# First two modulation vectors on TensorE in column tiles, and the order of work that follows from it

## The chip, the cores and the metric
The kernel runs on one core of a Trainium2 chip. The metric is the device time of one execution in microseconds (us). The engines are TensorE (PE for its matmuls, PEld for its weight loads), VectorE (DVE), ScalarE (ACT), GpSimd (POOL) and SyncE (SP), whose queue issues most transfers. Each engine works through its own instructions in order and waits on the others by semaphores.

## The reference, cut to what matters
One layer of a hybrid block over 1024 latent tokens and 256 context tokens, D = 1024, all in float32:

```
mods   = silu(c) @ ada_w + ada_b            # six vectors of 1024, for tokens; the same with c_ctx for the context
u      = rms_norm(x, ln1) * (1 + scale) + shift        # vectors 0 and 1; uc the same from ctx
z      = u @ w_in                            # S5, LRU, q, k, v, gates ... (5408 columns)
mixers : S5 scan, LRU (conv, two gated linear scans), GLA
out    : gated sum of branches @ w_out, residual, then norm, ConvFFN, residual, final norm
```

Vectors 0 and 1 are needed before the first projection can start, vectors 2 to 5 only after the mixers.

## The kernel before, in words
Everything is kept transposed: 128 channels on the partitions, tokens along the free axis, eight tiles k = 0 to 7 of 128 channels, and for the latent tokens two halves j of 512. Each float32 operand is split into a rounded part and a rest ("hi" and "lo", tiles `wh`/`wl` and `uh`/`ul`), and a product takes three matmuls: hi x hi, hi x lo, lo x hi.

**Start (lines 296 to 417, the table START on line 89).** The table is an order written out for all engines. Its steps: `x` loads half a tile of x (256 KB), `sq` squares it on ACT and adds it to a running sum, `rs` sums over channels on PE and takes the power -1/2, `rb` spreads the result over the partitions (line 272) and copies it to `rbc`. `a` loads 512 KB of `ada_w`; `ap` multiplies a block of 128 x 256 by one number of silu(c) and adds it up (L311, L313 on DVE, L307 and L309 on ACT and POOL); eight such products make the sums for the 128 channels of tile k, which `af` finishes on PE and DVE (L278, L318, L319). `xn` multiplies x by `rbc` (L381), `u` makes the hi part with scale and shift (L323) and writes the shifted x once more in full (L324), `ul` subtracts (L389). `g`/`gs` load and split the first weights. `m1`, `m2` and `mz` are the matmuls of three first blocks of 128 columns over all eight k and both halves (L395, L396, L402, and L283 to L285): 144 of 512 columns.

**Stream.** After that one generator, `proj_stream`, hands out all other projections. A `lat` block is 48 matmuls of 512 columns (L496 to L500), a `ctx` block 24 of 256. The call F(name) puts as many microseconds of the stream between two other pieces of PE's program as the table FILL says; `fill_until` runs it up to a marker. PE's order is that of the program; the other engines' order after the start is made by a scheduler from the dependencies.

**Context norm (lines 422 to 452).** The same norm for the context. The modulation of the context reads `ada_w` once more, and per k makes eight products on DVE, with 6 us of stream beside each k. Stream blocks handed out up to the marker "ctx": two gate blocks (lg), two q blocks, two g blocks.

**LRU (lines 899 to 964).** Two channel halves times two directions: six small matmuls each (L925), activations, scans, and per pass two rows of vectors 2 to 5: `ada_rows` (L474, 32 float32 matmuls of 32 x 128 in four column tiles), copied and turned into columns by `ada_cols` (L477, L483, L485). A row's weights are eight tiles of 256 KB, in one set of eight buffers. The stream gives k and v for the context and z; its marker "pc" ends the stage. Line 960 writes the LRU's result `yl`.

**S5 and on.** The S5 prologue on DVE, the decay logs of GLA, then S5, GLA, the merge, the FFN.

Of the kernel before, what the change touches and what calls it, by code (L numbers as in the profile page):

```python
# [20 lines left out]
KT = 8  # L21
# [17 lines left out]
def _parts(v, bits, n):  # L39
    out = []  # L40
    for _ in range(n):
# [21 lines left out]
FILL = {'ctx_a': [6.11],  # L63
        'ctx_b': [5.72],
        'ctx_k': [6.02, 6.02, 6.02, 6.02, 5.84, 6.02, 5.84, 6.02],
        'lru_a': [5.66],
        'lru_b': [1.42, 1.42, 1.34, 1.38, 1.04, 1.42, 1.48, 1.55, 1.42, 1.42, 1.38, 1.73, 1.42, 1.42, 1.42, 1.42, 1.78, 2.22, 1.42, 1.8, 1.42, 1.42, 1.92, 1.42],
# [19 lines left out]
ONPOOL = [('ap', 0, 3), ('ap', 0, 5), ('ap', 0, 6), ('ap', 1, 2), ('ap', 2, 7), ('ap', 3, 0), ('ap', 5, 3), ('ap', 7, 0), ('sq', 4, 0), ('sq', 5, 0), ('sq', 5, 1), ('sq', 6, 0), ('sq', 6, 1), ('xn', 0, 0), ('xn', 1, 0), ('xn', 2, 0), ('xn', 2, 1), ('xn', 5, 1), ('xn', 6, 0), ('xn', 7, 0), ('xn', 7, 1)]  # L87
ONDVE = [('ul', 6, 0), ('ul', 6, 1), ('ul', 7, 0), ('ul', 7, 1)]
START = [('x', 2, 1), ('x', 0, 0), ('sq', 0, 0), ('x', 5, 0), ('sq', 5, 0), ('x', 3, 0), ('sq', 3, 0), ('x', 4, 0), ('sq', 4, 0), ('x', 1, 0), ('sq', 1, 0), ('x', 7, 0), ('sq', 7, 0), ('x', 2, 0), ('sq', 2, 0), ('a', 0, 0), ('ap', 0, 0), ('ap', 0, 2), ('x', 6, 0), ('sq', 6, 0), ('ap', 0, 1), ('a', 0, 1), ('ap', 0, 4), ('a', 1, 0), ('ap', 0, 7), ('ap', 0, 6), ('ap', 0, 3), ('x', 1, 1), ('g', 0), ('x', 0, 1), ('x', 5, 1), ('ap', 0, 5), ('x', 3, 1), ('x', 4, 1), ('ap', 1, 0), ('ap', 1, 1), ('a', 1, 1), ('x', 6, 1), ('rs', 0), ('ap', 1, 2), ('g', 1), ('x', 7, 1), ('gs', 0, 0), ('gs', 0, 1), ('sq', 0, 1), ('sq', 1, 1), ('sq', 2, 1), ('sq', 4, 1), ('sq', 5, 1), ('ap', 1, 6), ('ap', 1, 4), ('af', 0), ('ap', 1, 3), ('sq', 6, 1), ('ap', 1, 7), ('rb', 0), ('xn', 0, 0), ('ap', 1, 5), ('sq', 3, 1), ('sq', 7, 1), ('a', 2, 0), ('a', 2, 1), ('ap', 2, 0), ('ap', 2, 2), ('ap', 2, 3), ('ap', 2, 1), ('ap', 2, 5), ('a', 3, 0), ('a', 3, 1), ('a', 4, 0), ('af', 1), ('ap', 2, 4), ('gs', 1, 0), ('gs', 0, 2), ('g', 2), ('gs', 1, 2), ('u', 0, 0), ('ul', 0, 0), ('a', 4, 1), ('rs', 1), ('ap', 2, 6), ('m1', 0, 0), ('a', 5, 0), ('xn', 1, 0), ('ap', 3, 0), ('ap', 3, 7), ('ap', 3, 5), ('ap', 3, 2), ('ap', 2, 7), ('a', 5, 1), ('gs', 1, 1), ('rb', 1), ('xn', 3, 0), ('m2', 0, 0), ('xn', 2, 0), ('af', 2), ('ap', 3, 4), ('xn', 2, 1), ('xn', 5, 0), ('ap', 3, 1), ('xn', 0, 1), ('u', 1, 0), ('m1', 1, 0), ('ul', 1, 0), ('u', 2, 0), ('ul', 2, 0), ('m1', 2, 0), ('ap', 3, 6), ('xn', 3, 1), ('u', 0, 1), ('m1', 0, 1), ('ul', 0, 1), ('m2', 2, 0), ('xn', 1, 1), ('u', 1, 1), ('ul', 1, 1), ('ap', 3, 3), ('a', 6, 0), ('a', 6, 1), ('ap', 4, 0), ('ap', 4, 5), ('ap', 4, 6), ('ap', 4, 7), ('ap', 4, 1), ('u', 2, 1), ('ul', 2, 1), ('af', 3), ('u', 3, 0), ('xn', 5, 1), ('ap', 4, 3), ('ap', 5, 0), ('ap', 5, 6), ('ap', 5, 1), ('ap', 5, 5), ('ap', 4, 4), ('ap', 5, 3), ('ul', 3, 0), ('xn', 4, 0), ('m2', 0, 1), ('gs', 2, 0), ('gs', 2, 2), ('u', 3, 1), ('ul', 3, 1), ('gs', 2, 1), ('m1', 1, 1), ('m1', 2, 1), ('m2', 2, 1), ('m2', 1, 1), ('ap', 4, 2), ('a', 7, 0), ('a', 7, 1), ('af', 4), ('u', 4, 0), ('xn', 4, 1), ('u', 4, 1), ('ap', 5, 7), ('m1', 3, 1), ('m1', 3, 0), ('m2', 3, 0), ('ap', 5, 4), ('ul', 4, 1), ('xn', 6, 1), ('ap', 5, 2), ('af', 5), ('u', 5, 0), ('m1', 4, 0), ('m2', 3, 1), ('ap', 6, 0), ('ap', 6, 4), ('ap', 6, 5), ('ap', 6, 2), ('m1', 5, 0), ('ap', 6, 7), ('m1', 4, 1), ('ap', 6, 6), ('ul', 4, 0), ('ap', 6, 3), ('ap', 6, 1), ('af', 6), ('ul', 5, 0), ('m2', 5, 0), ('m2', 1, 0), ('u', 5, 1), ('m1', 5, 1), ('ap', 7, 0), ('ap', 7, 7), ('ap', 7, 3), ('ap', 7, 1), ('ap', 7, 5), ('ap', 7, 6), ('xn', 6, 0), ('m2', 4, 0), ('ap', 7, 2), ('ul', 5, 1), ('g', 3), ('gs', 3, 0), ('gs', 3, 1), ('gs', 3, 2), ('u', 6, 0), ('m1', 6, 0), ('ap', 7, 4), ('af', 7), ('u', 6, 1), ('ul', 6, 1), ('m1', 6, 1), ('m2', 4, 1), ('m2', 6, 1), ('ul', 6, 0), ('m2', 6, 0), ('m2', 5, 1), ('xn', 7, 0), ('u', 7, 0), ('xn', 7, 1), ('u', 7, 1), ('ul', 7, 0), ('ul', 7, 1), ('mz',)]
# [22 lines left out]
def tile_kernel(tc, I, out, dbg=None):  # L112
# [140 lines left out]


# [39 lines left out]
    aws, raws, accs1, acs, dgs = {}, {}, {}, {}, {}  # L294

    def ada_load(k, i):

        aw = t0([128, 4, 256], "aw", 6)
        SY.dma_start(aw.rearrange("p k m -> p (k m)"), I["ada01"][k][:, i * 1024:(i + 1) * 1024])
        return aw  # L300

    def ada_prod(ac, kk, src, col, via):

        c = cs[:, kk, col:col + 1]
        if via:
            t = ac if kk == 0 else t0([128, 256], "at", 2)
            S.activation(t, src, AF.Copy, scale=c)  # L307
            if kk:
                G.tensor_tensor(ac, ac, t, OP.add)  # L309
        elif kk == 0:  # L310
            V.tensor_scalar(ac, src, c, None, OP.mult)  # L311
        else:
            V.scalar_tensor_tensor(ac, src, c, ac, OP.mult, OP.add)  # L313

    def ada_fin(k, ac, col, p):

        sums(p, ac, 2, 2 * k)
        V.scalar_tensor_tensor(mods[:, k, col, 0:1], p[:, 2 * k:2 * k + 1], ab1[:, k:k + 1], vc("ln1", k), OP.add, OP.mult)  # L318
        V.tensor_tensor(mods[:, k, col, 1:2], p[:, 2 * k + 1:2 * k + 2], vc("adab", k), OP.add)  # L319

    def u_hi(k, xk, col, oh):

        S.activation(oh, xk, AF.Identity, scale=mods[:, k, col, 0:1], bias=mods[:, k, col, 1:2])  # L323
        S.activation(xk, xk, AF.Identity, scale=mods[:, k, col, 0:1], bias=mods[:, k, col, 1:2])  # L324
# [4 lines left out]
    class Start:  # L329
# [4 lines left out]
        @staticmethod  # L334
        def a(k, i):
            aws[k, i] = ada_load(k, i)

        @staticmethod
        def g(kp):
            raws[kp] = wraw(I["g1"][kp])  # L340

        @staticmethod
        def gs(kp, b):
            sl = slice(kp * 256, (kp + 1) * 256)
            h, l = g1[b]
            split(h[:, sl], l[:, sl], raws[kp][:, b * 256:(b + 1) * 256])

        @staticmethod
        def sq(k, j):
            if k == 0:  # L350
                accs1[j] = t0([128, 512], "sqa", 1)
                S.activation(accs1[j], xs[k][:, tl[j]], AF.Square)
                return
            t = t0([128, 512], "sq", 2)
            S.activation(t, xs[k][:, tl[j]], AF.Square)
            (G if ("sq", k, j) in ONPOOL else V).tensor_tensor(accs1[j], accs1[j], t, OP.add)

        @staticmethod
        def rs(j):
            st = st2[:, 8 * j:8 * j + 4]  # L360
            sums(st, accs1[j], 4, by=per_d)
            dgs[j] = rstd_cols(st, 4)

        @staticmethod
        def rb(j):
            bcast(gps[2][j], dgs[j], 4)
            S.copy(rbc[:, tl[j]], gps[2][j])

        @staticmethod
        def ap(k, kk):  # L370
            if kk == 0:
                acs[k] = t0([128, 256], "ac", 3)
            ada_prod(acs[k], kk, aws[k, kk // 4][:, kk % 4], 0, ("ap", k, kk) in ONPOOL)

        @staticmethod
        def af(k):
            ada_fin(k, acs[k], 0, psm)

        @staticmethod
        def xn(k, j):  # L380
            (G if ("xn", k, j) in ONPOOL else V).tensor_tensor(xs[k][:, tl[j]], xs[k][:, tl[j]], rbc[:, tl[j]], OP.mult)  # L381

# [4 lines left out]
        @staticmethod  # L387
        def ul(k, j):
            (V if ("ul", k, j) in ONDVE else G).tensor_tensor(ul[j][:, k], xs[k][:, tl[j]], f32(uh[j][:, k]), OP.subtract)  # L389

# [31 lines left out]
    def ctx_norm():  # L422
        xc = t0([128, KT, 256], "xc")
        SY.dma_start(xc, I["ctx"].rearrange("p (k t) -> p k t", k=KT))
        acc = t0([128, 512], "sqa", 1)[:, :256]
        S.activation(acc, xc[:, 0], AF.Square)
        for k in range(1, KT):
            sq = t0([128, 512], "sq", 2)[:, :256]
            S.activation(sq, xc[:, k], AF.Square)
            V.tensor_tensor(acc, acc, sq, OP.add)  # L430
# [9 lines left out]
        p = sm()  # L440
        for k in range(KT):
            aw = [ada_load(k, i) for i in range(2)]
            ac = t0([128, 256], "ac", 3)
            for kk in range(KT):
                ada_prod(ac, kk, aw[kk // 4][:, kk % 4], 1, kk == 0)
# [265 lines left out]
    def proj_stream():  # L711
# [5 lines left out]
        for b in range(2):  # L717
            yield from lat(lambda p: out_rows(p, qsp[b]))
# [1541 lines left out]
```

## Time and profile before

| what | value |
|---|---|
| median of 3 runs | 1659.66 us (1659.45 to 1661.09) |
| profiled execution | 1658.82 us |
| its span in the trace | 1657.0 us |
| TensorE, granted clock, mean over the span | 0.977 |
| PE busy | 1543.8 us (93%) |
| DVE busy | 1157.1 us (70%) |
| ACT busy | 791.2 us (48%) |
| POOL busy | 550.4 us (33%) |

The time of an execution lies 1.8 us above the span, which runs from the first instruction to the last. A timeline row has its start, its length (for a merged row the length of all), engine, line, operation, what it writes and reads, the count, and the idle time before it with what ended it. Matmuls of one row run into one another, so the distance between two starts is the cost of one, and the length given is longer.

### The profile page before, as it was taken

The numbers are of one execution on the slowest core, as the hardware profiler recorded it, in microseconds if no ns is written. First come the engines' busy times: TensorE is split into PE (matmuls) and PEld (weight loads), VectorE is DVE, ScalarE is ACT, GpSimd is POOL, SyncE is SP. The second block draws the span as 40 slices with busy tenths as digits, with TensorE's granted clock in tenths as the row PEclk, the third lists the DMA queues.
The fourth block names the chain that finished last, engine by engine and source line by source line (L and its number), as shares of the span: only waits on it lengthen the run. The fifth ranks groups of instructions, "written<-read, shape, count | busy, mean of one in ns | idle before, by whom it ended". The sixth has DMA issues, their size and how long they took to land. (4 is left out here: it accounts for less than half of the span.)

```text
span 1657.0 us, 21399 instructions
## 1 busy us (share of the span) xinstructions
PE 1543.8 (93%) x7944; PEld 1259.4 (76%) x7944; DVE 1157.1 (70%) x1696; ACT 791.2 (48%) x1259; POOL 550.4 (33%) x349
## 2 busy tenths in 40 slices
PE   3799989979999999999999988999999999789997
PEld 2588855778887788788888767878788788578887
DVE  6874557978985715533461689888888887898862
ACT  4543566665553544442232555444444444334562
POOL 6732411342112422222236525333333333630023
PEclk9899999989999999999999999999999999899999
DMA  8464584232214143231374421222222224674312
GB/s 299 153 214 159 170 291 154 89 109 80 67 57 137 67 143 116 88 83 58 135 245 152 139 70 46 92 79 77 78 97 80 77 77 164 226 269 143 100 33 102
DMA packets 93784, 207.81 MB, mean 125 GB/s; under 512 B 13488, under 2 KB 34864, under 8 KB 93552
## 3 DMA queue, kind: packets, MB, share of 16 engines
q1 hardware_dynamic: 81968, 190.53, 34.8%
q10 hardware_dynamic: 11712, 15.91, 2.8%
q8 instruction: 62, 1.02, 0.3%
q14 instruction: 42, 0.34, 0.1%
HBM read 167.89 MB, written 38.52 MB: 125 GB/s over the span
## 5 line engine op out<-in xcount | busy, mean ns | idle before, releaser
L217 POOL TENSOR_TENSOR wl<-wr,wh 128x1024 fp32r<-128x1024 f32 (+2 forms) x99 | 199.3, 2017 | 393.4 <-ACT wh L216 346.8
L217 POOL TENSOR_TENSOR wp<-tmp,wp 128x512 fp32r<-128x512 f32 x44 | 73.9, 1699 | 229.7 <-ACT wp L216 196.6
L216 ACT CAST wh<-wr 128x1024 fp32r<-128x1024 f32 (+2 forms) x99 | 81.4, 830 | 132.9 <-PE mb L498 40.2
L496 PE MATMUL ma<-uh,wh 128*128 128x512 f32 x272 | 115.0, 423 | 4.7 <-ACT pt L763 4.7
L496 PE MATMUL mb<-uh,wh 128*128 128x512 f32 x272 | 107.2, 394 | 0.0
L498 PE MATMUL ma<-ul,wh 128*128 128x512 f32 x272 | 106.9, 393 | 0.0
L498 PE MATMUL mb<-ul,wh 128*128 128x512 f32 x272 | 106.8, 393 | 0.0
L500 PE MATMUL mb<-uh,wl 128*128 128x512 f32 x272 | 106.6, 392 | 0.0
L500 PE MATMUL ma<-uh,wl 128*128 128x512 f32 x272 | 106.4, 391 | 0.0
L216 ACT CAST wp<-tmp 128x512 fp32r<-128x512 f32 x78 | 46.4, 619 | 104.5 <-DVE tmp L1598 104.0
L217 POOL TENSOR_TENSOR wp<-wr,wp 128x512 fp32r<-128x512 f32 x44 | 81.9, 1872 | 40.3 <-ACT wp L216 40.3
L313 DVE SCALAR_TENSOR_TENSOR t<-t,c,t 128x256 f32<-128x256 f32 x106 | 74.5, 720 | 7.1 <-ACT t L307 4.9
L216 ACT CAST wp<-hd 128x512 fp32r<-128x512 f32 x88 | 51.7, 617 | 57.7 <-PE bkd L1961 40.0
L1662 DVE SCALAR_TENSOR_TENSOR ca<-gv,vec,ca 128x1023 f32<-128x1023 f32 (+2 forms) x66 | 62.0, 964 | 23.7 <-ACT ca L1654 23.6
L1665 DVE SCALAR_TENSOR_TENSOR ca<-gv,vec,ca 128x1023 f32<-128x1023 f32 (+2 forms) x66 | 73.1, 1132 | 0.0
L216 ACT CAST wp<-wr 128x512 fp32r<-128x512 f32 x97 | 57.4, 620 | 32.3 <-DVE wr L2003 9.6
L217 DVE TENSOR_TENSOR wp<-hd,wp 128x512 fp32r<-128x512 f32 x88 | 60.1, 710 | 18.1 <-ACT wp L216 18.1
L496 PEld LDWEIGHTS ma<-uh,wh 128*128 128x128 f32 x272 | 51.6, 190 | 18.9 <-ACT pt L763 6.0
L498 PEld LDWEIGHTS ma<-ul,wh 128*128 128x128 f32 x272 | 51.5, 189 | 11.3
L500 PEld LDWEIGHTS ma<-uh,wl 128*128 128x128 f32 x272 | 51.4, 189 | 11.4
L498 PEld LDWEIGHTS mb<-ul,wh 128*128 128x128 f32 x272 | 51.4, 189 | 11.3
L500 PEld LDWEIGHTS mb<-uh,wl 128*128 128x128 f32 x272 | 51.3, 189 | 11.3
(630 smaller groups left out, 4753.1 us busy)
## 6 DMA issues: line engine op xcount, KB each, us to landing
wr<-in_wup_dram SPq DMA_DIRECT2D x46, 512.0 KB
wr<-in_win_dram SPq DMA_DIRECT2D x40, 512.0 KB
t<-in_ada_dram SPq DMA_DIRECT2D x32, 512.0 KB
wa<-in_ada_dram SPq DMA_DIRECT2D x64, 256.0 KB
wr<-in_wdn_dram SPq DMA_DIRECT2D x22, 512.0 KB
hd<-hid SPq DMA_DIRECT2D x22, 512.0 KB
hid<-ca SPq DMA_DIRECT2D x21, 512.0 KB
wr<-in_wout_dram SPq DMA_DIRECT2D x16, 512.0 KB
```

The lines of the kernel that those rows point to most:

```text
L216: S.copy(h, src)
L217: lo.tensor_tensor(l, src, f32(h), OP.subtract)
L313: V.scalar_tensor_tensor(ac, src, c, ac, OP.mult, OP.add)
L496: PE.matmul(p[j], h[:, kk], uh[j][:, k], start=f, stop=False)
L498: PE.matmul(p[j], h[:, kk], ul[j][:, k], start=False, stop=False)
L500: PE.matmul(p[j], l[:, kk], uh[j][:, k], start=False, stop=e)
L1662: V.scalar_tensor_tensor(a[:, t0_ + 1:t0_ + 1 + n1], x[:, o:o + n1], fw[0], a[:, t0_ + 1:t0_ + 1 + n1], OP.mult, OP.add)
L1665: V.scalar_tensor_tensor(a[:, t0_ + c - 1:t0_ + n - 1], x[:, o + c:o + n], fw[2], a[:, t0_ + c - 1:t0_ + n - 1], OP.mult, OP.add)
```

## The change
The modulation of the first two vectors is taken out of DVE. `ada_w`'s first 2048 columns are laid out as four rows r = 0 to 3 of 512 columns, each row for two tiles k. A row is eight loads of 256 KB and 32 matmuls in four column tiles, as for the vectors 2 to 5, with the tokens' and the context's silu(c) side by side as two of the 32 columns. So one read of the weights serves both. Steps: `a` loads, `ar` multiplies, `at` copies to SBUF, `ac` turns rows into columns, `am` adds the constants. The weights of even rows go to a pool `paw` that lives on to the end of the LRU, those of odd rows below 8 to `p0`, which ends with the context norm.

x is multiplied by `rbc` and by the scale in one instruction (`un`, L315, DVE), `u` adds the shift alone, on ACT, and `ul` adds the shift and subtracts in one instruction (L321, DVE); the write-back of x by ACT is gone. START and FILL are new.

Rows 4 to 11 (vectors 2 to 5) start in the context norm: one after every second k, then one per pass of the LRU. The two q blocks move from the part before the marker "ctx" to the part between "lru" and "pc".

```diff
-FILL = {'ctx_a': [6.11],
-        'ctx_k': [6.02, 6.02, 6.02, 6.02, 5.84, 6.02, 5.84, 6.02],
+FILL = {'ctx_a': [6.0],
+        'ctx_k': [2.7, 2.7, 2.7, 2.7, 2.7, 2.7, 2.7, 2.7],
...
+    def ada_part(r, k):
+
+        w = (p0_ if r < 8 and r % 2 else paw_).tile([128, 512], F32, name=nm("wa"), tag="wa", bufs=8)
+        SY.dma_start(w, (I["ada01"][r] if r < 4 else I["ada25"][r - 4])[:, k * 512:(k + 1) * 512])
+        ada.setdefault(r, []).append(w)
+
+    def ada_rows(r, p):
+
+
+        for k, w in enumerate(ada.pop(r)):
+            for j in range(4):
+                PE.matmul(p[32 * j:32 * j + 32], c32[:, k], w[:, j * 128:(j + 1) * 128],
+                          start=(k == 0), stop=(k == KT - 1), skip_group_check=True)
+
+    def u_scaled(k, xk, col, rs):
+        V.scalar_tensor_tensor(xk, xk, mods[:, k, col, 0:1], rs, OP.mult, OP.mult)
...
-        S.activation(oh, xk, AF.Identity, scale=mods[:, k, col, 0:1], bias=mods[:, k, col, 1:2])
-        S.activation(xk, xk, AF.Identity, scale=mods[:, k, col, 0:1], bias=mods[:, k, col, 1:2])
+        S.activation(oh, xk, AF.Identity, bias=mods[:, k, col, 1:2])
+
+    def u_lo(k, xk, col, oh, ol):
+        V.scalar_tensor_tensor(ol, xk, mods[:, k, col, 1:2], f32(oh), OP.add, OP.subtract)
...
-            ac = t0([128, 256], "ac", 3)
-            for kk in range(KT):
-                ada_prod(ac, kk, aw[kk // 4][:, kk % 4], 1, kk == 0)
+            u_scaled(k, xc[:, k], 1, rbcc)
+            u_hi(k, xc[:, k], 1, uch[:, k])
+            u_lo(k, xc[:, k], 1, uch[:, k], ucl[:, k])
             F("ctx_k")
-            ada_fin(k, ac, 1, p)
-            V.tensor_tensor(xc[:, k], xc[:, k], rbcc, OP.mult)
-            u_hi(k, xc[:, k], 1, uch[:, k])
-            G.tensor_tensor(ucl[:, k], xc[:, k], f32(uch[:, k]), OP.subtract)
+            if k % 2:
+                ada_next()
...
         for f in range(2):
             yield from lat(lg_out)
         for b in range(2):
-            yield from lat(lambda p: out_rows(p, qsp[b]))
-        for b in range(2):
             yield from lat(lambda p: g_out(b, p))
         yield from marker("ctx")
...
         yield from marker("lru")
+        for b in range(2):
+            yield from lat(lambda p: out_rows(p, qsp[b]))
...
-                if mods_rows:
-                    ada_cols(*mods_rows)
-                r = 4 * f + 2 * d + a
-                mods_rows = r, ada_rows(r)
+                if a == 0:
+                    ada_next()
```

PE's order at the start, before: `ones` and `over_d` rows are sums over channels (of a tile's modulation, of the squares), `con,tmp` spreads the norm, and the rows with `uh`, `ul` are `m1` and `m2`.

```order
L278 MATMUL sm_122<-over_d,t_143 128x1 x4
L278 MATMUL sm_123<-ones,t_171 128x1 x2
L272 MATMUL sm_128<-con,tmp_211 128x128 x4
L278 MATMUL sm_123<-ones,t_201 128x1 x2
L278 MATMUL sm_122<-over_d,t_224 128x1 x4
L395 MATMUL ma_124<-uh_109,wh_130 128x512
```

The same engine now, from the sums of the second half on; `wa` is a tile of a row, `c_97` silu(c).

```order
L280 MATMUL sm_125<-over_d,t_243 128x1 x4
L311 MATMUL sm_126<-wa_308,c_97 32x128 x4
...
L274 MATMUL sm_132<-con,t_359 128x128 x4
L346 MATMUL sm_125<-con,t_369 128x8
L311 MATMUL sm_126<-wa_381,c_97 32x128 x4
...
L311 MATMUL sm_126<-wa_395,c_97 32x128 x4
L429 MATMUL mb_128<-uh_110,wh_133 128x512
```

The first matmuls of the second half (`mb` from `uh_110`) now stand behind the sums of the squares, the whole row r = 1 and the whole row r = 2.

DVE in the middle of the start, before, where products for the modulation (L313) stand between those of x (L381):

```order
L381 TENSOR_TENSOR x_94<-x_94,t_136 128x512
L313 SCALAR_TENSOR_TENSOR t_313<-t_272,c_97,t_313 128x256
L381 TENSOR_TENSOR x_89<-x_89,t_136 128x512
L313 SCALAR_TENSOR_TENSOR t_313<-t_274,c_97,t_313 128x256
L381 TENSOR_TENSOR x_92<-x_92,t_136 128x512
```

And now, behind the first constants of r = 1 (`mods`):

```order
L362 TENSOR_TENSOR mods<-sm_125,vec 128x4
L315 SCALAR_TENSOR_TENSOR x_89<-x_89,mods,t_139 128x512
L315 SCALAR_TENSOR_TENSOR x_90<-x_90,mods,t_139 128x512
L315 SCALAR_TENSOR_TENSOR x_91<-x_91,mods,t_139 128x512
L321 SCALAR_TENSOR_TENSOR ul_112<-x_89,mods,uh_110 128x512
L321 SCALAR_TENSOR_TENSOR ul_112<-x_90,mods,uh_110 128x512
L342 COPY t_446<-sm_126 128x128
```

The products are gone, and all 16 `un` and all 16 `ul` are DVE's; POOL keeps the splits of the weights and three sums.

SP's queue in the LRU stage, before (`wr` from `in_wv` or `in_win` is a block of the stream, `wa` a tile of a row):

```order
L207 DMA wr_1677<-in_wv_dram 128x1024
L207 DMA wr_1813<-in_wz_dram 128x256
L207 DMA wr_2433<-in_win_dram 128x1024
L466 DMA wa_1642<-in_ada_dram 128x512
```

And now around the rows r = 9 (its first and last tile) and r = 10 (its first and last):

```order
L206 DMA wr_1773<-in_wv_dram 128x1024
L303 DMA wa_1190<-in_ada_dram 128x512
...
L303 DMA wa_1204<-in_ada_dram 128x512
L206 DMA wr_1810<-in_wv_dram 128x1024
L303 DMA wa_1604<-in_ada_dram 128x512
...
L303 DMA wa_1618<-in_ada_dram 128x512
L206 DMA wr_1871<-in_wv_dram 128x1024
```

The second and third v block stand behind whole rows that wait for the buffers of the row before them; before, all four v blocks stood ahead of the second row.

## Rows read from the trace of the kernel before

**Rows 1.** The page's 40 slices: PE's busy tenths.
```profile
PE   3799989979999999999999988999999999789997
```
**Rows 2.** By stretch: PE, PEld, DVE, ACT, POOL busy (count), PEclk, DMA share, GB/s.
```profile
0.00:93.95 93.95, 53.76 (x208) 43.85 (x209) 75.16 (x130) 51.32 (x91) 58.00 (x65) 0.95 0.65 224
93.95:186.37 92.42, 92.42 (x474) 78.88 (x473) 46.47 (x84) 35.81 (x55) 36.38 (x20) 1.00 0.58 188
186.37:264.16 77.79, 69.57 (x770) 48.47 (x769) 48.20 (x43) 54.75 (x66) 20.67 (x8) 0.93 0.74 250
```
**Rows 3.** Waits of PE, 0 to 98 us: total, times, longest.
```profile
PE sm L278 <- DVE t L313: 17.2, 4, 6.9
PE sm L278 <- POOL t L356: 15.7, 1, 15.7
```
**Rows 4.** By stretch as in Rows 2: transfers (last two columns), PE's clock.
```profile
0.00:10.00 10.00, 0.00 (x0) 0.00 (x0) 3.55 (x20) 4.21 (x8) 2.62 (x19) 1.00 0.84 275
18.00:27.00 9.00, 3.06 (x12) 2.71 (x12) 5.95 (x10) 6.18 (x12) 8.05 (x9) 1.00 1.04 405
255.00:258.00 3.00, 2.98 (x26) 1.24 (x19) 2.72 (x3) 1.80 (x3) 0.00 (x0) 0.50 1.01 365
```
**Rows 5.** Timeline of ACT and PE in the start.
```profile
6.17 0.63 ACT L352 ACTIVATE t<-x 128x512 f32<-128x512 f32 x1 [2.27 <-DMA x<-in_x_dram]
28.92 0.81 ACT L323 ACTIVATE uh<-x,mods 128x512 fp32r<-128x512 f32 x1
...
15.69 1.87 PE L278 MATMUL sm<-over_d,t 128*128 128x1 f32 x8 [15.69 <-POOL t L356]
21.05 2.08 PE L272 MATMUL sm<-con,tmp 128*128 128x128 f32 x8
```
**Rows 6.** Timeline of PE: matmuls of 512 columns, slow, fast, in the stream.
```profile
35.05 0.63 PE L395 MATMUL ma<-uh,wh 128*128 128x512 f32 x1
35.48 0.63 PE L396 MATMUL ma<-uh,wl 128*128 128x512 f32 x1
...
83.30 0.39 PE L396 MATMUL ma<-uh,wl 128*128 128x512 f32 x1
83.52 0.39 PE L395 MATMUL sm<-uh,wh 128*128 128x512 f32 x1
...
93.95 0.40 PE L496 MATMUL ma<-uh,w 128*128 128x512 f32 x1
...
99.56 0.40 PE L496 MATMUL ma<-uh,w 128*128 128x512 f32 x1
```
**Rows 7.** Timeline of PE: sums, rows and columns of the modulation, stream again.
```profile
67.86 0.50 PE L278 MATMUL sm<-ones,t 128*128 128x1 f32 x4
...
198.48 1.95 PE L474 MATMUL sm<-wa,c 128*32 128x128 f32 x64
...
210.31 2.68 PE L474 MATMUL sm<-wa,c 128*32 128x128 f32 x32 [0.60 <-DMA wa<-in_ada_dram]
...
230.77 0.28 PE L483 MATMUL sm<-con,tmp 128*128 128x4 f32 x2
...
264.16 0.48 PE L496 MATMUL ma<-uh,wh 128*128 128x512 f32 x1
```
**Rows 8.** Timeline of DVE, and of POOL (one row).
```profile
70.91 4.36 DVE L313 SCALAR_TENSOR_TENSOR t<-t,c,t 128x256 f32<-128x256 f32 x3
86.05 1.28 DVE L389 TENSOR_TENSOR ul<-x,uh 128x512 fp32r<-128x512 f32 x2
90.75 5.64 DVE L313 SCALAR_TENSOR_TENSOR t<-t,c,t 128x256 f32<-128x256 f32 x14
277.17 1.98 DVE L960 SCALAR_TENSOR_TENSOR yl<-lt,lg 128x1024 f32<-128x1024 f32 x1
...
72.11 1.47 POOL L381 TENSOR_TENSOR x<-x,t 128x512 f32<-128x512 f32 x1
```
**Rows 9.** Waits of PE, 90 to 420 us: total, times, longest.
```profile
PE sm L474 <- DMA wa<-in_ada_dram: 7.3, 14, 1.4
```

## What the change does to the time: the prediction
> **What bounds the kernel now.** I read the 40 slices first: PE is busy in nine tenths or more of most of the program, three tenths of the first 41 us and seven of the second [rows 1]. So work that is off PE is worth little except where PE stands still. The table by stretch gives the place: up to 93.95 us, when the first stream block starts, PE is busy 53.8 us, a good part of that at half speed; from there to 186.37, where the LRU part of the stream begins, it has no idle time at all; from there to 264.16, the end of that part, it lacks 8.2 us and its granted clock is 0.93 [rows 2]. The waits say what it lacks in the start: 17.2 us for products of the modulation on DVE, 15.7 for the first sums of squares [rows 3]. DVE is busy 75 of the 94 us, POOL 58. So the start is bound by DVE with POOL beside it, and everything after it up to 264 by PE; of the LRU stage's idle time, 7.3 us are waits for the weights of the modulation rows [rows 9].
>
> **The change, part by part.** *The start.* DVE loses 64 products and PE the small sums; what is late next? I follow the data. The queue's order is x's first half, row 0, g, x's second half, row 1, g, row 2, g, row 3. Up to row 2's last tile that is 16 tiles of x and 24 of rows at 262 KB, two pieces of g at 393 KB and 0.33 MB of constants: 11.6 MB. In the first 10 us 2.75 MB moved; loads of 512 KB went at 405 GB/s, loads like a row's tiles, alone, at 365 [rows 4]. I take 350: 10 + 8.85/0.35 = 35.3 us, and 1.5 us more from moved to usable, since the first square starts at 6.17 although by the rates some 0.4 MB more than its tile had moved [rows 5]. So row 2 is in at 36.8, row 1 at 29.7, x's second half at 23.7, row 3 at 43.9.
>
> PE's order makes this the path: the second half's first matmuls stand behind the sums, row 1, the spread and row 2. By about 24.4 the first half of k = 0 is ready (its scale hangs on row 0, in at 16.6), and PE does two sets of nine matmuls, slowly, until 32. Then sums 1 us (cold eight took 1.87 [rows 5]), row 1 2 us, spread 1 to 2, copy, product and u (0.81) give 39; row 2's matmuls end at 39 too. From there 14 sets of nine are left for PE, at 0.227 us a matmul [rows 6]: 28.6. Row 3 is 32 matmuls, 1.95 [rows 7], two column steps 0.6. A cold PE issues at 0.43 [rows 6]; I let 15 matmuls go so, 3 us (bounds 0 and 4 from the pace; were all 126 slow, 25). Sum: the start ends at 39 + 28.6 + 2 + 0.6 + 3 = 73.2 instead of 93.95.
>
> Does DVE keep up? From 41 it has 11 `un` and 12 `ul` left. The trace has no such instruction of two full tiles; a DVE subtraction of 512 takes 0.64, 256-wide products 0.40 undisturbed (14 in 5.64) and 1.45 beside a busy POOL (3 in 4.36) [rows 8]. The near row is the subtraction, since POOL has only seven instructions left, about 8 us: 23 x 0.7 + 1.2 small ones = 17, end 58, nine us before PE wants the last tile at 69. At 1.45 each it would be 76: the upper end.
>
> *POOL and DVE.* Three DVE products took 4.36 us while POOL ran one instruction of 1.47 after another [rows 8]: DVE got one through per POOL instruction. "SBUF — State Buffer" of the Trainium skill, section "SBUF: two separate sides", says that a DVE instruction with two SBUF inputs and a POOL instruction lock each other out for their whole length, which speaks against moving `un` and `ul` to DVE. The trace agrees with it here; by it DVE would need 17 + 8 = 25 us from 41, end at 66, and the sum would stay as it is.
>
> *Stream up to the LRU.* 92.4 us before, all PE [rows 2]. Two q blocks leave: 24 matmuls take 5.61 [rows 6], so 96 take 22.4. Four rows come in: 1.95 and 0.21 for the columns [rows 7], 8.7. The small sums go: 0.36 to 0.5 each [rows 7], eight, 3. New: 75.7. The context's norm no longer needs its 6 us of cover per k: two DVE instructions and one on ACT per tile, some 1 us against 2.7. The context is the seventh thing in the queue after row 3 (g, a weight block, rows 4 and 5): 5.9 MB more at 350 GB/s, in at 61, before 73.
>
> *LRU.* 77.8 before [rows 2]. Plus the two q blocks 22.4, minus four rows 8.7, minus the idle 8.2 (rows are then asked for a pass ahead, and k, v and q fill the gaps), minus half speed: a clock of 0.93 is 14% of the time at half, which is 5.4 of work lost. New: 77.9. The LRU's own chain has 87 us in before (192.7 to 279.2) and as much room now; its last line ends 15 us after PE's part [rows 7, 8], and from there the S5 prologue runs on DVE as before. From the middle of that prologue on all engines have the same instructions in the same order.
>
> Sum: 20.8 from the start, 16.7 from the stream, nothing from the LRU: 37 us. 1658.8 - 37 = 1621.8 for the profiled execution; the median lies 0.8 above it, so 1622.
>
> *Size of transfers.* Loads of 256 KB alone moved 365 GB/s, those of 512 KB 405 [rows 4]. "DMA: Bandwidth & Descriptors" of the Trainium skill, section "Bandwidth", gives 138 GB/s at 64 KB and 341 at 1 MB and wants a megabyte per transfer; between them I estimate 240 for 256 KB. By that row 2 would be in at 48 and the total at 1633. The trace disagrees, by the 365.
>
> **The rivals.** *The start stays late*, for one of three reasons: DVE takes PE's place (1.45 an instruction, last tile at 76, start over at 80), or the queue moves 290 GB/s (row 2 at 42, start over at 78.5), or rows run at the cold price (32 in 2.68, twice that for 64 [rows 7]: 3.4 more each for rows 2 and 3, over at 80). For it: POOL's contention is in the trace. Against: each has slack of some us. Time 1627 to 1629.
>
> *SP's one queue holds up the stream.* Rows 8 to 11 share one set of buffers, so a row is only asked for when PE is done with the one before, and v blocks queue behind it. If PE comes to the v block first, it waits for 2.1 MB: 6 us at 350 GB/s. Against: row 9 is asked for some 13 us into the LRU stage, and the second v block is wanted some 30 us later. Rows 9 to 11 late, 18 us: 1640.
>
> *Slower.* The same mechanism from row 6 on: six rows at 6 us and 1.5 for landing are 45 us, more than the 37 gained: 1667. It decides from 6.2 us a row, which means that PE finds no row and no block ready each time. Against: six blocks lie between two rows' use in the context part.
>
> *It doesn't do what it says:* a product per column tile might not run beside its neighbours. Against: the same form of 32 matmuls takes 1.95 already [rows 7].
>
> **How the numbers follow.** Forecast (start over at 68 to 76, rest as summed): 0.62, its own range 1614 to 1626. Late start: 0.22. Transfers at 405 and no cold stretch (row 2 at 33.5, start over at 67, 1615) lies in the first. Rows 9 to 11 late: 0.09. Slower: 0.04. Nothing gained, because the LRU chain or the S5 prologue ends last whatever comes before: 0.03. The range runs from 1610, transfers at their best and the LRU's end 1.5 us earlier, plus small gains that I left out, to 1638. About 0.2% (3.3 us) can be told from no change. Faster 0.94, the same 0.02, slower 0.04.
>
> **What would show it.** The first stream block starts between 68 and 76; row 2's last tile is used near 39; PE has no gap above 2 us from there to the LRU's end; the LRU part is 76 to 80 long with two more blocks in it; the waits for `wa` are gone. Wrong would be: DVE behind PE in the second half of the start, PE waiting for POOL or ACT on a weight block in the LRU, or the LRU's last line more than 20 us behind PE's part.

## The result and the profile after

The changed kernel takes 1620.74 us (median of 4 runs, 1618.11 to 1621.14) against 1660.38 (4 runs, 1659.45 to 1661.76): ratio 0.977, 95% interval 0.9752 to 0.9785. Its profiled execution took 1620.94 us with a span of 1619.1, so it gains 37.9 us on the profiled execution of before. 1622 was predicted.

PE's busy tenths in 40 slices, which answer to [rows 1]: the first is now five tenths, the second full.

```profile
PE   5999999799998999999999998999999999789997
```

The three stretches of [rows 2] at their new limits (columns as there): up to the first stream block, to the marker "lru", to the end of PE's part of the LRU.

```profile
0.00:69.83 69.83, 50.53 (x441) 42.21 (x441) 41.67 (x87) 33.50 (x64) 20.11 (x37) 0.95 0.87 309
69.83:145.64 75.81, 75.81 (x608) 64.81 (x606) 17.94 (x34) 23.87 (x36) 22.09 (x10) 1.00 0.58 186
145.64:226.44 80.80, 76.11 (x604) 59.25 (x603) 43.76 (x36) 57.40 (x69) 26.21 (x9) 0.98 0.47 152
```

They took 93.95, 92.42 and 77.79 before. The start is 24.1 shorter (predicted 20.8), the stream 16.6 (16.7), the LRU part 3.0 longer (0.1), which is also just beyond the 76 to 80 that was given as a sign. DVE is down from 75 to 42 us in the start.

PE's waits in the start (to 72 us) answer to [rows 3]: the waits for DVE's products are gone, and after 25 us there is none above 1 us.

```profile
PE sm L280 <- DVE sp L899: 11.7, 1, 11.7
PE ma L429 <- ACT uh L318: 4.7, 1, 4.7
PE sm L274 <- POOL t L403: 1.4, 1, 1.4
PE sm L346 <- DVE t L342: 1.4, 2, 0.9
PE mb L429 <- ACT uh L318: 0.2, 1, 0.2
```

PE's waits from 145 to 420 us answer to [rows 9]: those for `wa` are gone. L692 is new. The second profile of the kernel before has L1246's wait too (2.5 us), and the second one of the changed kernel lacks L1188's, so these two come and go. The other three stood in before too, at 3.2 to 5.5 us.

```profile
PE ma L727 <- ACT wh L215: 7.6, 1, 7.6
PE ma L692 <- DVE wh L689: 3.9, 1, 3.9
PE sm L654 <- ACT tmp L661: 3.7, 2, 2.8
PE sm L1246 <- DVE s L1231: 2.8, 2, 2.5
PE ma L728 <- POOL wl L216: 2.5, 1, 2.5
PE sm L1188 <- DVE s L1222: 2.1, 1, 2.1
```

L692 is inside the LRU part. The split of z's weights waits on ACT behind the next pass of the LRU (L969, L959) and on DVE behind L970; PE starts z at 208.93, and from 209.9 to 213.3 its 256-wide matmuls come 0.21 us apart instead of 0.12, with a granted clock of 0.50 in that stretch (timelines of ACT, DVE, PE):

```profile
205.75 1.27 ACT L969 ACTIVATE lw<-la 128x1280 f32<-128x1280 f32 x1
206.92 0.68 ACT L959 ACTIVATE lt<-sm,hba 128x512 f32<-128x512 f32 x1
207.49 0.41 ACT L688 CAST wh<-wr 128x256 fp32r<-128x256 f32 x1
...
207.05 1.49 DVE L970 SCALAR_TENSOR_TENSOR lw<-lw,lt 128x1280 f32<-128x1280 f32 x1 [0.40 <-ACT lw L969]
208.46 0.42 DVE L689 TENSOR_TENSOR wh<-wr,wh 128x256 fp32r<-128x256 f32 x1
...
208.93 0.33 PE L692 MATMUL ma<-uch,wh 128*64 128x256 f32 x1 [3.86 <-DVE wh L689]
...
212.47 0.41 PE L692 MATMUL ma<-uch,wh 128*64 128x256 f32 x1
212.69 0.41 PE L693 MATMUL ma<-ucl,wh 128*64 128x256 f32 x1
```

Now follow one lead through the program: the same PE instruction in both traces, before minus after. At the first k block behind the LRU it is 264.16 - 226.44 = 37.7 us, near the 37 predicted. At the first 512-wide matmul on the S5's tiles (`sm` from `s`; called the S5's output below) it is 536.38 - 507.92 = 28.5. At the end it is 37.9. So in these two profiles 9 us were lost between 226 and 508 and came back later. Here are the rows, PE of before and of after:

```profile
536.38 0.50 PE L283 MATMUL sm<-s,s 128*128 128x512 f32 x1 [0.76 <-ACT s L220]
```
```profile
226.44 0.48 PE L529 MATMUL ma<-uh,wh 128*128 128x512 f32 x1
...
507.92 0.50 PE L285 MATMUL sm<-s,s 128*128 128x512 f32 x1 [1.35 <-ACT s L219]
```

What stands between them on DVE is the LRU's last line `yl` (it ended at 279.15 before, [rows 8]), and then the S5 prologue, for which DVE is busy 39.5 of the 40 us from 250 to 290 (the windows' row). The timeline of DVE, with POOL's row beside `yl`:

```profile
244.37 3.96 DVE L991 SCALAR_TENSOR_TENSOR yl<-lt,lg 128x1024 f32<-128x1024 f32 x1
...
244.09 2.51 POOL L216 TENSOR_TENSOR wl<-wr,wh 128x1024 fp32r<-128x1024 f32 x1 [9.42 <-ACT wh L215]
...
250.00:290.00 40.00, 37.21 (x242) 31.84 (x242) 39.50 (x113) 28.62 (x45) 12.46 (x8) 0.96 0.34 111
```

`yl` ends at 248.33, 30.8 us earlier than before, and 21.9 behind PE's part (226.44), where it was 15.0 behind.

How DVE gets from `yl` to its next lines is not the same in the two kernels. It needs `lsw` from ACT, and in ACT's order the cast of `yl` to `yb` stands ahead of that. Before (ACT, then DVE):

```profile
277.70 0.59 ACT L542 COPY pt<-ma 128x512 f32<-128x512 f32 x1 [1.83 <-PE ma L500]
...
279.86 1.05 ACT L216 CAST yb<-yl 128x1024 fp32r<-128x1024 f32 x1
...
281.47 2.46 DVE L630 SCALAR_TENSOR_TENSOR lsw<-lsw 128x512 f32<-128x512 f32 x1 [2.28 <-ACT lsw L629]
```

After:

```profile
248.36 1.04 ACT L215 CAST yb<-yl 128x1024 fp32r<-128x1024 f32 x1 [2.70 <-DVE s L1031]
...
249.97 2.48 DVE L663 SCALAR_TENSOR_TENSOR lsw<-lsw 128x512 f32<-128x512 f32 x1 [1.61 <-ACT lsw L662]
```

Before, ACT was still busy behind a copy that had waited for PE's block when `yl` ended (279.15), so PE let DVE go on, and `yl` had 0.7 us to spare. After, ACT idles 2.70 us until `yl` is there (L1031 is the small instruction right behind it). In the three further profiles of the program before (below, two of them with its inputs in another order) `yl` has 3.2 us to spare once and is waited for twice, 0.7 and 0.8 us; in the two further ones of the changed program ACT waits 2.7 us for it. The two were level before, and the change put `yl` last.

So there are two accounts: PE's lead of 37.7, or `yl`'s of 30.8. T1 in the runs below says that `yl` counts, T2 that PE does.

### The profile page after: what moved, and what is told of

Read it like the earlier page. It is cut to its first block, busy times and chain, and to the rows that moved or that the text cites. A ratio compares the mean times of both kernels' runs of the same rounds, so it can differ in the third digit from the quotient of the medians.

```text
span 1619.1 us, 21583 instructions
## 1 busy us (share of the span) xinstructions
PE 1527.9 (94%) x8144; PEld 1256.8 (78%) x8144; DVE 1095.1 (68%) x1598; ACT 770.0 (48%) x1221; POOL 504.8 (31%) x313
## 5 line engine op out<-in xcount | busy, mean ns | idle before, releaser
L216 POOL TENSOR_TENSOR wl<-wr,wh 128x1024 fp32r<-128x1024 f32 (+2 forms) x87 | 183.3, 2109 | 455.5 <-ACT wh L215 428.2
L215 ACT CAST wh<-wr 128x1024 fp32r<-128x1024 f32 (+2 forms) x87 | 77.3, 891 | 140.4 <-issue 42.0
L533 PEld LDWEIGHTS mb<-uh,wl 128*128 128x128 f32 x272 | 51.3, 189 | 11.4
L529 PEld LDWEIGHTS mb<-uh,wh 128*128 128x128 f32 x272 | 51.7, 190 | 9.7 <-issue 1.4
```

The source lines that it names most:

```text
L215: S.copy(h, src)
L216: lo.tensor_tensor(l, src, f32(h), OP.subtract)
L529: PE.matmul(p[j], h[:, kk], uh[j][:, k], start=f, stop=False)
L533: PE.matmul(p[j], l[:, kk], uh[j][:, k], start=False, stop=e)
```

## The experiments

**The move of the q blocks undone.**

```diff
-        wsrc.extend([win[i] for i in (2, 7, 8)])
+        wsrc.extend([win[i] for i in (2, 5, 6, 7, 8)])
         for f in range(2):
             yield from lat(lg_out)
+        for b in range(2):
+            yield from lat(lambda p: out_rows(p, qsp[b]))
...
         yield from marker("lru")
-        for b in range(2):
-            yield from lat(lambda p: out_rows(p, qsp[b]))
```

> The changed kernel with the two q blocks again ahead of the marker ctx. Theory T1 (the LRU's last line yl, through the S5 prologue and scan on DVE, sets where PE stands at about 400 us): the LRU's first gate matmul comes some 20.6 us later, its chain is again as short as before (86 us instead of 94.5), so yl ends at 261 instead of 248, and the time is about 1633. Theory T2 (only PE's own sums count): PE's LRU part needs about 71.5 us from its first gate matmul, since waits fill what the q blocks filled, and ends at 246 instead of 226.4: about 1640. Theory T3 (the move is only another order of the same work): 1621.

1629.23 us (1623.85 to 1629.35; ratio to before 0.981, 0.9785 to 0.9833), 8.5 more than the changed kernel. `yl` (DVE), the first k block and the S5's matmul (PE):

```profile
257.77 1.92 DVE L991 SCALAR_TENSOR_TENSOR yl<-lt,lg 128x1024 f32<-128x1024 f32 x1
...
231.96 0.47 PE L529 MATMUL ma<-uh,wh 128*128 128x512 f32 x1
516.22 0.50 PE L285 MATMUL sm<-s,s 128*128 128x512 f32 x1 [1.88 <-ACT s L219]
```

PE's part ended at 232, not 246, so T2's number rested on a wrong estimate of its waits. `yl` ended at 259.7, near T1's 261 and 11.4 later than with the change; the time went up by 8.5, where T1 had 12. T3 is out: the move is worth some 7 to 8 us (against the second measurement of the changed kernel below, 7.4). Since PE's part ends 5.5 later as well, this run alone does not decide between T1 and T2.

**`yl` later, PE's stream untouched.**

```diff
         S.activation(z, z, AF.Tanh, scale=math.sqrt(2.0 / math.pi))
+        if f == 1:
+            for _ in range(12):
+                V.tensor_scalar(z, z, 1.0, 0.0, OP.mult, OP.add)
```

> The changed kernel with twelve extra DVE instructions (z times 1 plus 0, 1024 wide, 0.67 us each) on the LRU's chain just before its last lines; nothing else is added on PE. yl ends 7 to 8 us later. T1 (yl and DVE's S5 work behind it set PE's place at 400 us): with the slope of the run with the q blocks put back (yl 11.4 us later, time 8.3 later) 5 to 7 us more, 1626 to 1628. T2 (only PE's sums count): 1621.

1627.55 us (1626.08 to 1628.26; 0.981, 0.9792 to 0.9824). DVE and PE:

```profile
255.28 1.98 DVE L994 SCALAR_TENSOR_TENSOR yl<-lt,lg 128x1024 f32<-128x1024 f32 x1
...
226.49 0.47 PE L529 MATMUL ma<-uh,wh 128*128 128x512 f32 x1
514.61 0.49 PE L285 MATMUL sm<-s,s 128*128 128x512 f32 x1 [1.27 <-ACT s L219]
```

PE's part ends at the same place (226.49 against 226.44), `yl` 8.9 later, PE 6.7 later at the S5's output, the time 6.8 higher. T2 is refuted here and T1 holds: nothing was added on PE. What the run shows is the price of a later `yl` on DVE, about three quarters of the delay.

**`yl` earlier, PE's part later.**

```diff
-        'lru_b': [1.7, 1.7, 1.7, 1.7, 1.7, 1.7, 1.7, 1.7, 1.7, 1.7, 1.7, 1.7, 1.7, 1.7, 1.7, 1.7, 1.7, 1.7, 1.7, 1.7, 1.7, 1.7, 1.7, 1.7],
+        'lru_b': [1.0, 1.0, 1.0, 1.0, 1.0, 1.0, 1.0, 1.0, 1.0, 1.0, 1.0, 1.0, 1.0, 1.0, 1.0, 1.0, 1.0, 1.0, 1.0, 1.0, 1.0, 1.0, 1.0, 1.0],
```

> The changed kernel with 1.0 instead of 1.7 us of stream between two pieces of the LRU; the rest of the stream then follows the LRU's last piece. PE has the same work in this part. T1: each of the four passes gets up to 4.2 us shorter, yl ends 8 to 14 us earlier, PE's waits between 350 and 400 us shrink, and the time falls by 5 to 9.5 us, to 1611 to 1616. T2: PE's part has the same length, the time stays at 1621 within 1.5.

1615.13 us (1614.71 to 1619.26; 0.974, 0.9716 to 0.976). DVE and PE:

```profile
234.80 1.94 DVE L991 SCALAR_TENSOR_TENSOR yl<-lt,lg 128x1024 f32<-128x1024 f32 x1
...
233.82 0.79 PE L529 MATMUL ma<-uh,wh 128*128 128x512 f32 x1 [3.45 <-ACT lsw L696]
503.01 0.40 PE L285 MATMUL sm<-s,s 128*128 128x512 f32 x1
```

PE's part ends 7.4 us later than with the change and the kernel is faster all the same, since `yl` comes 11.6 earlier. But only 4.9 of these arrive at 503: there PE no longer waits for the S5's output (no wait stands on the row), so from here on another limit rules. T1's sign is there too: from 340 to 420 us PE waits for nothing, where the changed kernel has 4.9 us (L1246 and L1188 in the list above). To compare the two directly, both ran once more on one chip:

> The changed kernel once more, on one chip with the next run, to compare the two: 1619 to 1622.

> The version with 1.0 us of stream between the LRU's pieces, on the chip of the run before. T1: 3 to 7 us faster than the changed kernel, 1614 to 1617, with intervals that do not meet. T2: no difference.

The changed kernel took 1621.79 (1619.61 to 1623.58), this one 1616.90 (1614.27 to 1618.93). The ranges of the runs do not meet, though the intervals of the ratios to before (0.9763 to 0.9803, 0.9733 to 0.9774) overlap. It is some 5 us better than the changed kernel.

**z's weights split earlier.** The load and split of z's weights leave `z_steps` and are called from `v_steps` (the call alone is shown).

```diff
             ws = take(2)
+            if hv and len(blocks) == 2:
+                zl.append(z_load())
```

> The changed kernel; the load and the split of z's weights are written one v half earlier, so that ACT's cast does not stand behind the next pass of the LRU. T2: PE's wait of 3.9 us for the split and the 1.7 us lost at half speed behind it go, and the time falls by 5.6 to 1615. T1: the time falls only by what yl comes earlier, 2 to 5 us, as the passes behind it start earlier: 1616 to 1619. If neither, because something else ends last: 1621.

1616.68 us (1613.88 to 1619.16; 0.974, 0.9715 to 0.9767). The wait for the split is gone, but a new one stands almost in its place; PE, 145 to 420 us:

```profile
PE ma L703 <- ACT pt L739: 3.6, 1, 3.6
```

`yl` ends at 248.18, where it was. By T1 alone nothing should be gained; PE's gain at the S5's output is 1.7 us, and the rest arises behind it. Its runs spread over 5 us and overlap with those of the changed kernel (1618.11 to 1623.58 in two measurements), so a gain is not shown beyond noise: the time lies in T1's range, its reason (an earlier `yl`) did not happen.

**Both together.** The two edits above in one kernel.

> Both single edits that were faster than the changed kernel, together: z's weights split one v half earlier, and 1.0 us of stream between the LRU's pieces. T1: with 1.0 us the LRU's chain no longer waits for z, so the second edit adds little: yl at 236, 1613 to 1615. T2: both gains add up, 4 and 6 us: 1611.

1617.60 us (1615.36 to 1619.20; 0.975, 0.9735 to 0.9764), not below either of the two alone. `yl` ends at 235.76, PE reaches the S5's output at 500.11. T1 expected 1613 to 1615, T2 1611; neither holds: once `yl` is this early, its place tells little. PE is 2.9 us earlier at the S5's output than with 1.0 us of stream alone, but the rest of the program takes 1115.2 us, where that run took 1109.9; why is not shown.

**Loads of 512 KB.**

```diff
-        w = (p0_ if r < 8 and r % 2 else paw_).tile([128, 512], F32, name=nm("wa"), tag="wa", bufs=8)
+        if k % 2:
+            return
+        w = (p0_ if r < 8 and r % 2 else paw_).tile([128, 2, 512], F32, name=nm("wa"), tag="wa", bufs=4)
...
```

> The changed kernel with each row's weights in four loads of 512 KB instead of eight of 256 KB, in the same memory. If the rows' transfers bound the start anywhere (the rule that small transfers run far below the rate of large ones): row 2 comes 3 to 10 us earlier and the start ends as much earlier, 1611 to 1618. If, as the trace has it, PE waits for no row there: start and time are the same within 1.5 us, 1621.

1619.55 us (1616.54 to 1622.08; 0.976, 0.9746 to 0.9776). The start ends at 71.50, and in nine other profiles with the new start at 69.6 to 71.6. From 8 to 37 us the queue moved 353 GB/s, with loads of 256 KB 372. Row 2's last tile landed at 34.0 instead of 34.8, and PE came to that row only at 36.9 (35.2 in the changed kernel). "DMA: Bandwidth & Descriptors" of the Trainium skill, section "Bandwidth", asks for transfers of a megabyte, by rates of transfers issued from GpSimd; here, on SyncE's queue, doubling them to 512 KB gave nothing.

**The FFN.** The lead that came back arises in the FFN, where instructions and order are the same.

> The kernel before, unchanged, profiled once more. In the two traces at hand the FFN (PE's first matmul into bkd after 1059 us of the changed kernel, 1089 of before, up to the last norm's spread) takes 542.6 us with the change and 552.2 before, though its instructions are the same in the same order. Theory F1: this belongs to the kernel before; the part is again 552 within 1.5 us. Theory F2: it differs from run to run; the part differs from 552 by 3 us or more, and the span with it.

F1 holds: the part takes 550.8 us. Over all profiles it is 549.2 to 552.2 in the four of before and 541.0 to 545.8 in the ten with the change. In each of its loops a load of 512 KB of `w_up` is late for DVE, and takes longer before. One load in the trace of before, then after (SP's queue, then DVE; the row's end names the wait):

```profile
1140.90 0.33 SPq L207 DMA_DIRECT2D wr<-in_wup_dram  x1
...
1145.10 0.69 DVE L1598 TENSOR_TENSOR tmp<-wr 128x512 f32<-128x512 f32 x1 [1.90 <-DMA wr<-in_wup_dram]
```
```profile
1110.70 0.33 SPq L206 DMA_DIRECT2D wr<-in_wup_dram  x1
...
1114.07 0.69 DVE L1630 TENSOR_TENSOR tmp<-wr 128x512 f32<-128x512 f32 x1 [1.06 <-DMA wr<-in_wup_dram]
```

Issue to use, median over the 15 or 16 loads that DVE waits for: 4.09 us in the first profile of before and 4.08 in the second, 3.57 after, 3.43 to 3.55 in nine more profiles with the change. The loop's period is 19.60 and 19.60 against 18.94 to 19.08. Between 1060 and 1380 us of the kernel before, where these loops lie, PE's lead rises from 28.2 to 34.3; the other 4.4 us come behind them, up to 1500, and are not explained by these loads. I tried one cause for the loads, the place of the inputs in memory: `ada01` and `ada25` put last, then `con` and `mask` put first (of each edit the lines of one input).

```diff
-    o["ada25"] = con(ada[:, 2048:].reshape(8, 128, 8, 512).transpose(2, 1, 0, 3).reshape(8, 128, 4096))
...
     o["mask"] = con(dup((i64[None, :] < i64[:, None]).astype(np.int32)))
+    o["ada25"] = con(ada[:, 2048:].reshape(8, 128, 8, 512).transpose(2, 1, 0, 3).reshape(8, 128, 4096))
     return o
```

> The kernel before with its two inputs of ada_w put last in the list of inputs; no instruction changes. Theory F3 (where the FFN's inputs lie in device memory sets how long its 512 KB loads of w_up take): the time from the issue of such a load to its first use leaves 4.09 us, the period of 19.61 us shortens or lengthens by 0.3 or more, and the time moves by 6 us or more. Otherwise both stay, 1660, and the cause of the slower FFN stays open.

```diff
+    o["mask"] = con(dup((i64[None, :] < i64[:, None]).astype(np.int32)))
     o["x"] = con(ktiles(n["x"][0].T).reshape(128, -1))
...
-    o["mask"] = con(dup((i64[None, :] < i64[:, None]).astype(np.int32)))
     return o
```

> The kernel before with its two small inputs con and mask (178 KB) put first in the list of inputs instead of last, which shifts all others by an odd amount; no instruction changes. F3 (where the FFN's inputs lie sets how long its loads take): issue to use leaves 4.09 us or the period leaves 19.61 us by 0.3 or more. Otherwise as before, and the cause of the slower FFN stays open.

> The changed kernel with the same shift of its inputs. F3: the period of its FFN leaves 19.1 us, up to 19.6, and the time rises by up to 10 us. Otherwise 19.1 and 1621.

The loads took 4.11 and 4.10 us in the two kernels of before (period 19.63 and 19.64; one run each, 1655.61 and 1657.77), 3.54 in the changed one (19.07; 1619.55). These two shifts do nothing to the loads, and F3 falls as far as they test it. Why the same load is slower in the program of before stays open.

**`yl` and the S5's output in one table** (us, profiled execution):

| kernel | PE's LRU part ends | `yl` ends | S5's output on PE | distance from `yl` |
|---|---|---|---|---|
| before | 264.2 | 279.2 | 536.4 | 257.2 |
| before, second profile | 262.4 | 276.5 | 538.5 | 262.0 |
| before, `ada_w` last | 262.2 | 278.8 | 536.8 | 258.0 |
| before, `con` first | 263.6 | 280.2 | 538.2 | 258.0 |
| q blocks back | 232.0 | 259.7 | 516.2 | 256.5 |
| `yl` later | 226.5 | 257.3 | 514.6 | 257.4 |
| loads of 512 KB | 228.3 | 250.2 | 509.2 | 259.0 |
| changed | 226.4 | 248.3 | 507.9 | 259.6 |
| changed, second profile | 228.1 | 250.0 | 509.9 | 259.9 |
| changed, `con` first | 227.9 | 249.8 | 509.6 | 259.7 |
| z earlier | 228.9 | 248.2 | 506.3 | 258.1 |
| 1.0 us of stream | 233.8 | 236.7 | 503.0 | 266.3 |
| 1.0 us, second profile | 236.0 | 239.0 | 503.3 | 264.4 |
| both | 232.8 | 235.8 | 500.1 | 264.4 |

While `yl` moves by 32 us, the distance stays at 256 to 260, but for the second profile of before (262.0); there ACT reached the cast 3.2 us after `yl` had ended, so PE's block and not `yl` let DVE go on. From the end of PE's part the distance to the S5's output runs from 267 to 288. Only with `yl` 9 to 12 us earlier still does the distance from `yl` grow. Profiles of one kernel differ by some 2 us: over the four of before and the three of the changed kernel the mean lead is 35.6 us at the end of PE's part, 29.2 at `yl`, 28.3 at the S5's output and 37.1 at the end. The loss is then 7 us and the gain behind it 9.

## Why the prediction was right, and where it was not

The time was right (1622, measured 1620.7), and so were the two large terms. The way from them to the total was not: a loss of 7 to 9 us and a gain of 9, neither of which I had seen, cancelled. That the total came out so close is luck.

*The start*: 73.2 predicted, 69.83 measured, on the path that was named: PE runs without a wait above 1 us from the second half's first matmul on. Two terms were too large. That matmul stood at 37.35, not 39: the queue moved 372 GB/s instead of the 350 that I took, row 2 was in at 34.8, and PE came to it without a wait at 35.2. And the 3 us of cold matmuls were not there (the clock was 1.00 from 32 to the end of the start). The rest of the sum, 31.2 us behind that matmul, was short by 1.3. In the second profile of the changed kernel that matmul stood at 38.5 and the start ended at 71.0, so about 1 us of this is spread. DVE kept up: its last `ul` ended at 60.1, five us before PE wanted it, where I had 58; many of its `un` and `ul` took 0.74 us, near the 0.7 that I had taken. The late start did not come.

*The stream*: 75.7 predicted, 75.81 measured. The context's norm cost nothing with 2.7 us of cover.

*The LRU part*: 77.9 predicted, 80.80 measured. The waits for `wa` went, as said. New is the wait of 3.86 us for z's weights with 3.4 us at half speed behind it. I had named a PE that waits for a weight block in the LRU, and a gap above 2 us, as signs of error, but gave them no price. None of rows 9 to 11 was late. PE's part ended at 226.4, predicted 226.8, since the shorter start made up for it.

*The step that failed* is that the LRU's chain has "87 us in before (192.7 to 279.2) and as much room now; its last line ends 15 us after PE's part", and with it the sum, which adds up PE's stretches alone. From the first gate matmul (153.8) the chain took 94.5 us, and `yl` came 21.9 us behind PE's part, beyond the 20 that I had set as the sign of error. The run with a later `yl` shows that it counts: PE's part unchanged, 6.8 us lost. So it was not PE's 37.7 that reached the S5's output but 28.5, near `yl`'s 30.8. What made the LRU's chain longer is partly what I called free: the two q blocks in it, and the stream between its pieces. With the q blocks back it takes 83.3 us, with 1.0 us of stream 84.5, and z's wait lies in it too. Another part may be POOL: the chain's 28 DVE instructions themselves took 51.2 us instead of 46.3, since more of them ran beside a POOL instruction (see the last section). But in the run with 1.0 us of stream they took 52.0 and the chain was short all the same, so that gain came from the time between them. How the 8 us divide is not shown. A case in which the LRU chain or the S5 prologue ends last stood among the rivals, with 0.03 and "nothing gained". It holds as a limit and not as a full stop: `yl` itself moved by 30.8, since the start and the stream ahead of it did.

*What paid it back* is mostly the FFN, some 7 to 10 us shorter, for a cause that no step of mine held and that the runs did not find. Without it the kernel would have come out at about 1629, inside the range and outside the likeliest case's own.

## What to carry to other kernels

A full PE is no proof that PE's sum sets the time: look behind the stage for the in-order engine that starts its next stage only after its last line of this one (here DVE, busy 39.5 of 40 us), and carry that line's time through the sum beside PE's. Where two paths arrive there level, as PE's block and `yl` did before, a change that speeds up one of them hands the place to the other. When work is moved in as cover for a chain, its pieces stand between the chain's own on the same engine: ask whether the chain grows, and whether less cover is better. And follow one instruction's lead through both traces to the end even where the total agrees, since terms can cancel.

## What the runs showed of the hardware

A DVE instruction with two tiles as inputs took as long beside a POOL instruction as if it waited for that to end. `yl` took 3.96 us when it started 0.28 us after POOL's `wl` of 2.51 us (the rows of the first section), and 1.98 where POOL was idle (the run with `yl` later): POOL's remaining 2.2 us and its own 1.9 make 4.1. In the second profile of the changed kernel it took 3.96 again. The Trainium skill says the same under "SBUF — State Buffer", section "SBUF: two separate sides": for a DVE instruction with two inputs in SBUF and a POOL instruction that reads SBUF, the lock holds for a whole instruction. Here it fell on the line that counts.

A load of 512 KB, on the same queue and among the same instructions, was used 4.1 us after its issue (median) in every profile of the program before and 3.4 to 3.6 us in every profile with the change. One of the 16 DMA engines is late with it: a load's landing is reported in 16 parts, and of the load of before shown above 15 had landed 3.41 us after its issue and the last at 4.11, of the one after all 16 by 3.28. The trace's single transfers of 4 KB, 128 to a load, show it for all loads: the longest of a load, which begins about 1 us after the issue, takes 1.00 to 1.13 us by the median in the four profiles of before and 0.64 to 0.68 in the ten with the change, while the median transfer takes 0.16 in both. What holds up that engine is not shown. In the transfers' own view of the two loads (to 6.1 us after the issue, 40 slices, GB/s) a store of 512 KB, issued 1.1 us behind the load, follows it. The load of before was used at 4.20 us, in the 28th slice; the tail at 27 GB/s behind that, a sixteenth of the peak of 430, belongs to the store, with one engine still behind the others:

```profile
GB/s 0 0 0 0 0 0 242 295 161 242 269 242 403 349 349 376 296 349 349 430 430 403 430 376 322 242 161 54 27 27 27 27 0 0 0 0 0 0 0 0
```
```profile
GB/s 0 0 0 0 0 0 242 349 161 269 430 295 376 430 403 242 349 376 403 349 430 430 430 403 269 134 107 0 0 0 0 0 0 0 0 0 0 0 0 0
```
